# Ordering the residual's renewal behind the last transposed-row difference in a two-layer hybrid decoder trunk

## The chip, the core and the metric

The kernel runs on one core of one Trainium2 chip. The metric is the device time of one launch in microseconds, and smaller is better. The kernel before the change takes 2078.81 us, the median of three runs (2078.62 to 2080.05).

## What is computed

The reference is a decoder trunk of two layers on one sequence of 512 tokens, 1024 wide. Each layer has three sub-layers: a feed-forward half step, a mixer, and another feed-forward half step. Every sub-layer has the same frame: its input rows are scaled and shifted by vectors that come from a conditioning vector, its output is gated and added to the residual, and the sum is normalised:

```
h = x * (1.0 + scale) + shift
y = swiglu(h, w1, w3, w2)            # or hybrid_mixer(h, ...)
x = layer_norm(ALPHA * x + weight * (1.0 + gate) * y, g, b)
```

The mixer projects h into the inputs of three head groups (sparse attention, a gated spatial unit, a state-space scan) and projects their joined outputs back. Every product of matrices is kept to float32 accuracy.

## The kernel before, in words

**Tiling.** The 512 tokens are four blocks of 128. The residual `x_sb` holds them with tokens on partitions. Matmuls want the contraction on partitions, so the scaled and shifted rows are kept transposed, and in two parts: `hT_hi`, rounded to the matmul's format, and `hT_lo`, the difference of the exact value and `hT_hi`. A float32 product is then three matmuls (`mm3`, L120 to L123): high by high, high by low, low by high. Weights are split in the same way after their load (L103 on ScalarE, L105 on VectorE).

**From one sub-layer to the next.** At the end of a sub-layer, each token block goes through `post_norm` (L247): the output is added to the residual and its statistics are taken (L244, L245, L258, L232, L233, L260), and ScalarE writes the normalised block into a buffer `z` (L269). `flush` (L272) hands `z` to `spread` (L209): TensorE transposes it in eight pieces of 128x128 into two PSUM banks `hps` (L215), ScalarE scales and shifts seven of the pieces (L226) and VectorE one (L224) into `hsum`, ScalarE rounds to `hT_hi` (L228), and VectorE takes the difference `hT_lo` (L229). There are two differences of 128x512 per block, so eight per sub-layer. This way leads straight from `z` to the next sub-layer's input; the layer norm's own gain and offset are folded into the scale and shift.

**The renewal.** The residual itself still needs the layer norm's gain and offset. `renew` (L278 to L282) does this on VectorE for each block: a product `x = z * lg` (L281) and a sum `x = x + lb` (L282), each 128x1024 in float32. `renew` is called once at the end of a sub-layer, in the feed-forward step (L404) and in the mixer (L1026). The last sub-layer has none; it writes the output. So there are five boundaries between sub-layers, with 4 products and 4 sums each. The renewed residual is read again only when the next sub-layer's output is added to it.

**What sets the order.** A tile scheduler orders the instructions of each engine when the program is built, by dependences and priorities. Each engine then works off its list in order, and so does each queue of transfers. Where nothing says otherwise, the scheduler may put the renewal of one block between the steps of the others.

**The start of a mixer** (L460 to L486). For each of the four token blocks, two products go into two PSUM banks, `tA` (L465, 24 matmuls of 284 columns) and `tB` (L469, 24 matmuls of 256 columns). These banks come from a pool with three banks, taken in turn: the first block's `tA` and `tB` and the second block's `tA` have one each; the second block's `tB` takes the bank of the first `tA`, and the third block's `tA` takes the bank of the first `tB`. A bank can be taken again when its last reader is done. For `tB` that is the last step of the activation `gelu2`: ScalarE squares (L428), VectorE multiplies and adds (L429, L430), ScalarE takes tanh (L431), and VectorE writes `gv` (L432), reading `tB` once more. After the change VectorE's lines L429, L430, L432 are numbered L431, L432, L434.

**The start of a feed-forward step.** For each tile of the hidden width, two products `h` go into two PSUM banks. VectorE reads the first in L311 and the second in L312 (L313 and L314 after the change), which frees them for a later tile. VectorE also splits weights there (L105), reduces the next conditioning vectors (L156) and adds one to the gate `G` (L192). The buffers of `z`, `lg`, `lb` and `G` come from one pool of eight, and the load of the next `lg`, `lb` and `G` is issued on SyncE's queue when a buffer is free.

Of the kernel before, what the change touches and what calls it, by code (L numbers as in the profile page):

```python
# [10 lines left out]
F32 = mybir.dt.float32  # L11
# [40 lines left out]
def kernel(ctx: ExitStack, tc: tile.TileContext, a: dict, out: bass.AP,  # L52
                             subs=((0, 0), (0, 1), (0, 2), (1, 0), (1, 1), (1, 2))):
    nc = tc.nc
    V, S, G, PE = nc.vector, nc.scalar, nc.gpsimd, nc.tensor
# [18 lines left out]
    def slab(s, pool="s", dt=F32):  # L74
        return sp[pool].tile([128, 512], dt, tag=pool, name=nm(s))
# [8 lines left out]
    def bank(k, s):  # L84
        return psp[k].tile([128, 512], F32, tag=k, name=nm(s))
# [53 lines left out]
    hT_lo = const.tile([128, 4, 8, 128], F32R, name="hT_lo")  # L139
# [69 lines left out]
    def spread(b, z, P, banks):  # L209
        tiles = []  # L210
        for q in range(2):
            ps = bank(banks[q], "hps")
            for i in range(4):
                k = 4 * q + i
                PE.transpose(ps[:, i * 128:(i + 1) * 128], z[:, k * 128:(k + 1) * 128], ident)  # L215
            tiles.append(ps)
        for q in range(2):
            t = slab("hsum", "q")
            t3 = t.rearrange("p (k t) -> p k t", k=4)
            for i in range(4):  # L220
                sl = slice(i * 128, (i + 1) * 128)
                k = slice(4 * q + i, 4 * q + i + 1)
                if k.start in DVE_MOD:
                    V.tensor_scalar(t[:, sl], tiles[q][:, sl], P["GA"][:, k], P["BB"][:, k], op0=ALU.mult, op1=ALU.add)  # L224
                else:
                    S.activation(t[:, sl], tiles[q][:, sl], AF.Identity, bias=P["BB"][:, k], scale=P["GA"][:, k])  # L226
            hh = hT_hi[:, b, 4 * q:4 * q + 4, :]
            S.copy(hh, t3)  # L228
            V.tensor_sub(hT_lo[:, b, 4 * q:4 * q + 4, :], t3, hh.bitcast(F32))  # L229

    def rsqrt(dst, src, scale, eps, n):
        V.tensor_scalar(dst, src, scale, eps, op0=ALU.mult, op1=ALU.add)  # L232
# [39 lines left out]
    def flush(P, n=0):  # L272
        while len(P.get("z", [])) > n:
            b, z, banks = P["z"].pop(0)
            spread(b, z, P, banks)
            P.setdefault("zz", []).append((x_sb[:, b, :], z))

    def renew(P, n=0):  # L278
        while len(P.get("zz", [])) > n:
            x, z = P["zz"].pop(0)  # L280
            V.tensor_mul(x, z, P["lg"])  # L281
            V.tensor_add(x, x, P["lb"])  # L282

    def hT(t, b0, b1, k):
        return t[:, b0:b1, k, :]
# [11 lines left out]
    def ffn(l, s, P, last, bg, lead_order, params, feed=None):  # L297
# [21 lines left out]
        for half in range(2):  # L319
# [73 lines left out]
            for b in range(4):  # L393
# [6 lines left out]
                else:  # L400
                    flush(P)
                    post_norm(b, y[b], P, last, "YY")
        flush(P)
        renew(P)  # L404


# [27 lines left out]
    def mixer(l, P, last, lane, bg, gate_params, norm_params):  # L434
# [589 lines left out]
        tick(99)  # L1024
        flush(P)
        renew(P)  # L1026


# [90 lines left out]
    for n, (l, s) in enumerate(subs):  # L1119
        last = n == len(subs) - 1  # L1120
        P = {}
# [108 lines left out]
```

## Time and profile before

| what | value |
|---|---|
| median of three runs | 2078.81 us (2078.62 to 2080.05) |
| the profiled execution: its own time | 2078.53 us |
| the profiled execution: its span in the trace | 2076.8 us |
| TensorE (PE) busy | 2037.8 us, 98% |
| VectorE (DVE) busy | 1330.7 us, 64% |
| ScalarE (ACT) busy | 770.2 us, 37% |
| chain that ended last | PE 90%, DVE 5%, ACT 2%, issue 1%, DMA 1% |
| mean granted clock of PE | 0.998 |

The profiled execution took 2078.53 us; its trace spans 2076.8 us, and 1.7 us lie around it. In a row of the trace the engines are PE (TensorE matmul), PEld (weight load), DVE (VectorE), ACT (ScalarE), POOL (GpSimd) and SPq (SyncE's queue); L215 is line 215 of the kernel, and `hps<-cst,z` names what is written and what is read. In a timeline row the first number is the start, the second the duration, and square brackets give how long the engine stood idle before it, and for whom.

### The profile page before, as it was taken

Reading aid. Unit: us, or ns where it says so; the run is one execution under the profiler, and the core shown is the slowest. Engines: PE = TensorE matmul, PEld = TensorE weight load, DVE = VectorE, ACT = ScalarE, POOL = GpSimd, SP = SyncE. Lnnn points to the kernel's source line nnn. Section 1 sums busy time; section 2 is a strip of 40 time slices with the busy share of each in tenths; the row PEclk is TensorE's granted clock in tenths of the full one; section 3 lists DMA queues with packets and bytes.
Section 4 is the critical chain, followed back from the end, with each engine's and each line's share of the span. In section 5 each row is a group of like instructions: output and inputs, shape, how many; then the busy total and the mean of one; then the engine's idle time right before and its main releaser. Section 6 shows DMA issues by size and latency. Waiting matters only on the chain.

```text
span 2076.8 us, 25951 instructions
## 1 busy us (share of the span) xinstructions
PE 2037.8 (98%) x10024; PEld 1652.0 (80%) x10024; DVE 1330.7 (64%) x2425; ACT 770.2 (37%) x1352; POOL 27.8 (1%) x43
## 2 busy tenths in 40 slices
PE   6999999999999999999999999999999999999997
PEld 5888888887666888888888888888776678888886
DVE  6784455778898875334696534468788984444454
ACT  3321223525556422222343222235356673222322
POOL 0000000000000000000000000000000000000000
PEclk9999999999999999999999999999999999999999
DMA  9662633235353763332566333143254523233321
GB/s 359 225 232 83 213 122 124 74 99 173 126 169 92 260 201 108 93 100 61 172 231 185 93 100 98 65 144 102 92 172 129 176 79 125 81 112 93 100 92 41
DMA packets 93144, 280.26 MB, mean 135 GB/s; under 512 B 19251, under 2 KB 23603, under 8 KB 93020
## 3 DMA queue, kind: packets, MB, share of 16 engines
q1 hardware_dynamic: 92348, 275.95, 40.6%
q0 software_dynamic: 672, 2.64, 0.4%
q8 instruction: 79, 1.29, 0.3%
q14 instruction: 45, 0.37, 0.1%
HBM read 276.41 MB, written 4.76 MB: 135 GB/s over the span
## 4 chain that ended last, share of the span: by engine, by line
PE 90%; DVE 5%; ACT 2%; issue 1%; DMA 1%; POOL 0%; SPq 0%; POOLq 0%; ACTq 0%
PE h L121 15%; PE h L122 15%; PE h L123 15%; PE y L121 8%; PE y L123 8%; PE y L122 8%; PE pj L121 3%; PE pj L122 3%; PE pj L123 3%; PE op L931 3%; PE tp L921 2%; PE S L890 1%; DVE raw L156 1%; PE S L891 1%; PE hid L624 1%
## 5 line engine op out<-in xcount | busy, mean ns | idle before, releaser
L103 ACT CAST whi<-raw 128x1024 fp32r<-128x1024 f32 (+1 forms) x306 | 316.8, 1046 | 719.4 <-issue 353.8
L121 PE MATMUL h<-hT_hi,whi 128*128 128x512 f32 (+1 forms) x1488 | 559.1, 377 | 4.5 <-ACT hT_hi L1064 4.4
L122 PE MATMUL h<-hT_lo,whi 128*128 128x512 f32 (+1 forms) x1488 | 559.1, 376 | 0.0
L123 PE MATMUL h<-hT_hi,wlo 128*128 128x512 f32 (+1 forms) x1488 | 558.9, 376 | 0.0
L105 DVE TENSOR_TENSOR wlo<-raw,whi 128x1024 fp32r<-128x1024 f32 (+1 forms) x306 | 369.4, 1215 | 232.8 <-ACT whi L103 232.4
L121 PEld LDWEIGHTS h<-hT_hi,whi 128*128 128x128 f32 x1488 | 280.1, 188 | 56.0 <-ACT hT_hi L1064 5.4
L123 PEld LDWEIGHTS h<-hT_hi,wlo 128*128 128x128 f32 x1488 | 280.4, 188 | 50.8
L122 PEld LDWEIGHTS h<-hT_lo,whi 128*128 128x128 f32 x1488 | 280.5, 188 | 50.5 <-DVE hT_lo L1065 0.2
L121 PE MATMUL y<-whi,ghi 128*128 128x512 f32 x576 | 224.1, 389 | 0.0
L122 PE MATMUL y<-wlo,ghi 128*128 128x512 f32 x576 | 224.1, 389 | 0.0
L123 PE MATMUL y<-whi,glo 128*128 128x512 f32 x576 | 224.1, 389 | 0.0
L156 DVE CUSTOM_DVE_ANT_0 raw<-raw,csil 128x1024 f32<-128x1024 f32 x144 | 173.7, 1218 | 22.9 <-DMA raw<-in_ada_w_dram 22.4
L312 DVE TENSOR_TENSOR th<-th,h 128x512 f32<-128x512 f32 x88 | 60.2, 685 | 147.3 <-PE h L123 146.9
L101 DVE TENSOR_TENSOR raw<-raw,G 128x1024 f32<-128x1024 f32 x86 | 104.9, 1221 | 66.8 <-DMA raw<-in_w_dram 66.3
L123 PEld LDWEIGHTS y<-whi,glo 128*128 128x128 f32 x576 | 108.1, 188 | 22.5
L121 PEld LDWEIGHTS y<-whi,ghi 128*128 128x128 f32 x576 | 108.1, 188 | 22.5
L122 PEld LDWEIGHTS y<-wlo,ghi 128*128 128x128 f32 x576 | 108.1, 188 | 22.4
L121 PE MATMUL pj<-hT_hi,whi 128*128 128x512 f32 x288 | 117.3, 407 | 0.0
L122 PE MATMUL pj<-hT_lo,whi 128*128 128x512 f32 x288 | 113.7, 395 | 0.0
L123 PE MATMUL pj<-hT_hi,wlo 128*128 128x512 f32 x288 | 113.3, 393 | 0.0
L315 ACT CAST ghi<-th 128x512 fp32r<-128x512 f32 x88 | 54.5, 620 | 145.7 <-DVE th L312 145.7
L311 DVE SCALAR_TENSOR_TENSOR th<-th,h 128x512 f32<-128x512 f32 x88 | 59.9, 681 | 44.9 <-ACT th L310 44.8
(291 smaller groups left out, 2552.4 us busy)
## 6 DMA issues: line engine op xcount, KB each, us to landing
raw<-in_w_dram SPq DMA_DIRECT2D x264, 512.0 KB, 3.6
raw<-in_ada_w_dram SPq DMA_DIRECT2D x144, 512.0 KB, 5.5
raw<-in_wS_dram SPq DMA_DIRECT2D x36, 512.0 KB, 3.5
raw<-in_cw_dram SPq DMA_DIRECT2D x16, 512.0 KB, 3.7
raw<-in_wo_dram SPq DMA_DIRECT2D x16, 512.0 KB, 4.2
T<-lane SPq DMA_DIRECT2D x16, 256.0 KB, 3.7
lg<-in_ln_g_dram SPq DMA_DIRECT2D x6, 512.0 KB, 4.6
lb<-in_ln_b_dram SPq DMA_DIRECT2D x6, 512.0 KB, 3.8
```

What stands on the lines that cost most here:

```text
L101: V.tensor_mul(raw, raw, gain)
L103: S.copy(hi[:, :n], raw[:, :n])
L105: V.tensor_sub(lo[:, :n], raw[:, :n], hi[:, :n].bitcast(F32))
L121: PE.matmul(o, lh, rh, start=first, stop=False)
L122: PE.matmul(o, lh, rl, start=False, stop=False)
L123: PE.matmul(o, ll, rh, start=False, stop=last)
L156: V.tensor_tensor_reduce(out=raw, in0=raw, in1=cond["c"], scale=0.5, scalar=0.0, op0=ALU.mult, op1=ALU.add, accum_out=acc[:, k:k + 1])
L311: V.scalar_tensor_tensor(th, th, 1.0, h1, op0=ALU.add, op1=ALU.mult)
L312: freed[0] = V.tensor_mul(th, th, h3).ins
L315: S.copy(hi, th)
L921: PE.transpose(tp[0:n, e * 128:(e + 1) * 128], pr[e][:, kb * 128:kb * 128 + n], ident)
L931: PE.matmul(op[r, :], v, pt[0:n, g * 256:(g + 1) * 256], start=(br == 0), stop=(br == 2 and kb == qb))
```

## The change

The difference L229 now leaves its instruction in `P["turned"]`, so that after the last block the entry is the last difference of the sub-layer. `renew` puts its products and sums inside `tc.issue_after(P["turned"])`: in the order that the scheduler writes for VectorE they all stand behind that instruction. What is computed is the same, and no instruction is added.

```
-            V.tensor_sub(hT_lo[:, b, 4 * q:4 * q + 4, :], t3, hh.bitcast(F32))
+            P["turned"] = V.tensor_sub(hT_lo[:, b, 4 * q:4 * q + 4, :], t3, hh.bitcast(F32)).ins
...
     def renew(P, n=0):
-        while len(P.get("zz", [])) > n:
-            x, z = P["zz"].pop(0)
-            V.tensor_mul(x, z, P["lg"])
-            V.tensor_add(x, x, P["lb"])
+        if len(P.get("zz", [])) > n:
+            with tc.issue_after(P["turned"]):
+                while len(P["zz"]) > n:
+                    x, z = P["zz"].pop(0)
+                    V.tensor_mul(x, z, P["lg"])
+                    V.tensor_add(x, x, P["lb"])
```

VectorE's order at the start of the first layer's mixer, before. The numbers behind names count buffers: `z_2616`, `z_2676`, `z_2736` and `z_2796` are the four normalised blocks, `hsum_2823` is the second half of the last of them, and `gv_2881` with `tB_2885` belongs to the mixer's first token block.

```order
L281 TENSOR_TENSOR x_sb<-z_2736,lg_493 128x1024
L258 BN_AGGR mv_2795<-st_2794 128x2
L282 TENSOR_TENSOR x_sb<-x_sb,lb_494 128x1024
...
L281 TENSOR_TENSOR x_sb<-z_2796,lg_493 128x1024
L229 TENSOR_TENSOR hT_lo<-hsum_2787,hT_hi 128x512
L282 TENSOR_TENSOR x_sb<-x_sb,lb_494 128x1024
L229 TENSOR_TENSOR hT_lo<-hsum_2816,hT_hi 128x512
L224 TENSOR_SCALAR hsum_2823<-hps_2811,GA_1645,BB_1646 128x128
...
L229 TENSOR_TENSOR hT_lo<-hsum_2823,hT_hi 128x512
L432 SCALAR_TENSOR_TENSOR gv_2881<-gl_2938,tB_2885 128x256
```

The same place in the changed kernel:

```order
L229 TENSOR_TENSOR hT_lo<-hsum_2823,hT_hi 128x512
L283 TENSOR_TENSOR x_sb<-z_2616,lg_493 128x1024
L283 TENSOR_TENSOR x_sb<-z_2676,lg_493 128x1024
L284 TENSOR_TENSOR x_sb<-x_sb,lb_494 128x1024 x2
L283 TENSOR_TENSOR x_sb<-z_2736,lg_493 128x1024
L283 TENSOR_TENSOR x_sb<-z_2796,lg_493 128x1024
L284 TENSOR_TENSOR x_sb<-x_sb,lb_494 128x1024 x2
L434 SCALAR_TENSOR_TENSOR gv_2881<-gl_2938,tB_2885 128x256
```

The renewals of the four blocks, which stood between the steps of the normalisation and the differences, now stand in one piece behind the last difference, and ahead of the instruction that frees the first block's `tB`.

TensorE's order at the same place, as the difference of the two kernels (`y_2327` is the last output of the feed-forward step, `tA_2884` the mixer's first product, `z_2736` the third normalised block):

```order
 L122 MATMUL y_2327<-wsl_2585,ghi_2302 128x512
 L123 MATMUL y_2327<-wsh_2583,glo_2303 128x512
+L215 MATMUL hps_2770<-cst,z_2736 128x128 x4
+L215 MATMUL hps_2775<-cst,z_2736 128x128 x4
 L121 MATMUL tA_2884<-whi_2849,hT_hi 128x284
 L122 MATMUL tA_2884<-wlo_2851,hT_hi 128x284
...
-L215 MATMUL hps_2770<-cst,z_2736 128x128 x4
-L215 MATMUL hps_2775<-cst,z_2736 128x128 x4
```

The transposes of the third block move ahead of the first nine matmuls of `tA`.

VectorE's order at the start of the first layer's second feed-forward step, in the changed kernel (`hsum_5838` is the second half of the last block, `th_6085` with `h_1080_5877` and `h_1081_5878` the first hidden tile):

```order
L229 TENSOR_TENSOR hT_lo<-hsum_5838,hT_hi 128x512
L283 TENSOR_TENSOR x_sb<-z_5373,lg_4611 128x1024
L283 TENSOR_TENSOR x_sb<-z_5616,lg_4611 128x1024
L284 TENSOR_TENSOR x_sb<-x_sb,lb_4612 128x1024 x2
L283 TENSOR_TENSOR x_sb<-z_5749,lg_4611 128x1024
L283 TENSOR_TENSOR x_sb<-z_5811,lg_4611 128x1024
L284 TENSOR_TENSOR x_sb<-x_sb,lb_4612 128x1024 x2
L105 TENSOR_TENSOR wlo_6083<-raw_6079,whi_6081 128x1024
L313 SCALAR_TENSOR_TENSOR th_6085<-th_6085,h_1080_5877 128x512
L192 TENSOR_SCALAR G_6107<-G_6107 128x1024
L314 TENSOR_TENSOR th_6085<-th_6085,h_1081_5878 128x512
```

Before, none of the eight renewals stood behind the last difference here; `G` came directly behind it, and L312 followed five instructions later. GpSimd's order does not change.

## Rows read from the trace of the kernel before

**Rows 1.** The page, part 1: busy time, share of the span, instructions.

```profile
PE 2037.8 (98%) x10024; PEld 1652.0 (80%) x10024; DVE 1330.7 (64%) x2425; ACT 770.2 (37%) x1352; POOL 27.8 (1%) x43
```

**Rows 2.** Waits of PE: total us, times, longest us.

```profile
PE hps L215 <- ACT z L269: 4.1, 5, 1.4
```

**Rows 3.** Timeline of PE, first layer's mixer start (start, duration, engine, line).

```profile
386.00 0.29 PE L121 MATMUL tA<-whi,hT_hi 128*128 128x284 f32 x1
...
388.73 1.09 PE L215 MATMUL hps<-cst,z 128*128 128x128 f32 x8 [1.40 <-ACT z L269]
...
393.67 1.09 PE L215 MATMUL hps<-cst,z 128*128 128x128 f32 x8
...
401.55 0.30 PE L121 MATMUL tA<-whi,hT_hi 128*128 128x284 f32 x1
```

**Rows 4.** Timeline of DVE, the same stretch.

```profile
388.70 1.23 DVE L281 TENSOR_TENSOR x_sb<-z,lg 128x1024 f32<-128x1024 f32 x1
389.84 0.20 DVE L258 BATCH_NORM_AGGREGATE mv<-st 128x2 f32<-128x12 f32 x1
...
398.72 0.69 DVE L229 TENSOR_TENSOR hT_lo<-hsum,hT_hi 128x512 fp32r<-128x512 f32 x1
399.33 0.41 DVE L432 SCALAR_TENSOR_TENSOR gv<-gl,tB 128x256 f32<-128x256 f32 x1
```

**Rows 5.** Timeline of ACT, the same stretch.

```profile
389.42 1.86 ACT L226 ACTIVATE hsum<-hps,BB,GA 128x128 f32<-128x128 f32 x5 [0.52 <-PE hps L215]
```

**Rows 6.** The two renewal lines: count, shortest/median/longest ns, first and last start.

```profile
L281 DVE TENSOR_TENSOR x_sb<-z,lg x20: 1212/1224/1227, 372.1 to 1710.8; 128x1024 f32<-128x1024 f32 x20
...
L282 DVE TENSOR_TENSOR x_sb<-x_sb,lb x20: 1193/1214/1226, 373.8 to 1712.0; 128x1024 f32<-128x1024 f32 x20
```

**Rows 7.** Timeline of PE, second layer's mixer start.

```profile
1409.18 0.29 PE L121 MATMUL tA<-whi,hT_hi 128*128 128x284 f32 x1
...
1411.62 1.09 PE L215 MATMUL hps<-cst,z 128*128 128x128 f32 x8 [1.11 <-ACT z L269]
...
1424.44 0.30 PE L121 MATMUL tA<-whi,hT_hi 128*128 128x284 f32 x1
```

**Rows 8.** Windows at the end: stretch, length, PE, PEld, DVE, ACT, POOL, PEclk, DMA, GB/s.

```profile
2063.00:2064.00 1.00, 0.95 (x5) 0.45 (x3) 0.34 (x3) 0.07 (x1) 0.55 (x1) 1.00 0.23 86
...
2066.00:2067.00 1.00, 0.00 (x0) 0.00 (x0) 1.00 (x3) 0.00 (x0) 0.00 (x0) 0.86 0.00 0
2067.00:2068.00 1.00, 0.00 (x0) 0.00 (x0) 1.00 (x2) 0.00 (x0) 0.00 (x0) 0.50 0.22 82
```

**Rows 9.** Timeline of PE at the kernel's start.

```profile
15.39 1.22 PE L121 MATMUL h<-hT_hi,whi 128*128 128x512 f32 x2 [1.14 <-ACT hT_hi L1064]
...
17.69 0.63 PE L123 MATMUL h<-hT_hi,wlo 128*128 128x512 f32 x1
18.12 0.63 PE L121 MATMUL h<-hT_hi,whi 128*128 128x512 f32 x1
...
19.08 0.39 PE L121 MATMUL h<-hT_hi,whi 128*128 128x512 f32 x1
19.31 0.40 PE L122 MATMUL h<-hT_lo,whi 128*128 128x512 f32 x1
...
22.73 1.21 PE L121 MATMUL h<-hT_hi,whi 128*128 128x512 f32 x4 [2.35 <-ACT hT_hi L1064]
```

**Rows 10.** Timeline of PE, starts of the feed-forward steps behind the first mixer.

```profile
688.49 1.09 PE L215 MATMUL hps<-cst,z 128*128 128x128 f32 x8 [0.27 <-ACT z L269]
...
710.01 0.39 PE L121 MATMUL h<-hT_hi,whi 128*128 128x512 f32 x1
...
1046.15 1.09 PE L215 MATMUL hps<-cst,z 128*128 128x128 f32 x8 [1.09 <-ACT z L269]
```

**Rows 11.** Timeline of DVE, first layer's second feed-forward start.

```profile
694.58 0.69 DVE L229 TENSOR_TENSOR hT_lo<-hsum,hT_hi 128x512 fp32r<-128x512 f32 x1 [0.69 <-ACT hT_hi L228]
```

**Rows 12.** The page, part 6: a load's issue count, KB, us to landing.

```profile
lg<-in_ln_g_dram SPq DMA_DIRECT2D x6, 512.0 KB, 4.6
```

## The prediction, made before the changed kernel ran

> **What bounds the kernel now.** I read the page's busy times first: TensorE works 98% of the span [rows 1], so a change on VectorE can gain only where TensorE stands still for it, and can lose wherever it makes TensorE stand still. Then I read the waits of TensorE. Those that the renewal can touch are the transposes that wait for a normalised block: 4.1 us in five waits [rows 2], one at each boundary between sub-layers. The timelines of the boundaries show why: VectorE has a renewal of 1.22 us [rows 6] between the steps of the normalisation, so that `z` comes late. At the first mixer's start TensorE idles 1.40 us for it [rows 3], at the second mixer 1.11 us [rows 7], at the feed-forward start in the second layer 1.09 us [rows 10]; about 0.5 us is left for the other two, of which 0.27 us stands in the row at 688.49 [rows 10].
>
> **The change, part by part.** Nothing is added or removed: 20 products and 20 sums move, eight at each of five boundaries, all on VectorE; no transfer is moved by hand. Where they overlap, one starts 1.14 us behind the other (388.70 to 389.84 [rows 4]), so a piece of eight takes 8 x 1.14 = 9.1 us (by their full durations 9.8 us [rows 6]). The question is who is queued behind that piece.
>
> *First mixer.* Behind the piece stands `gv` (L432 before), the last reader of the first block's `tB` bank, and the third block's `tA` takes that bank. Before, `gv` ended at 399.33 + 0.41 = 399.74 [rows 4] and the third block began at 401.55 [rows 3], so the bank was free 1.8 us ahead of need. In the changed kernel:
> - TensorE turns the third normalised block right behind the last output, at 386.00, where `tA` began [rows 3], without the wait.
> - ScalarE began to scale that block at 389.42 [rows 5], 0.69 us behind the transposes at 388.73 [rows 3]; now at about 386.7. The last difference began at 398.72 [rows 4], 9.30 us behind the scaling. I keep that distance, since ScalarE's work on the two blocks and TensorE's matmuls between their transposes are the same: 386.7 + 9.3 = 396.0, done 0.6 us later (the next instruction started 0.61 us behind it [rows 4]), 396.6.
> - The piece: 396.6 + 9.1 = 405.7. Then `gv`, 0.41 us: 406.1, and the bank is free for TensorE at about 406.2.
> - Without a wait TensorE would have wanted it at 401.55 - 1.40 = 400.15 or a little sooner. So it stands still some 6 us, and the third block starts 406.2 - 401.55 = 4.65 us later than before.
>
> Nothing gives this back: TensorE has no other work ahead of that matmul, and the blocks behind follow in order. While it waits VectorE and ScalarE catch up, so I see no second wait behind it.
>
> *Second mixer.* The same list, later. `tA` began at 1409.18, the third block at 1424.44 [rows 7]. With the same distances, 1409.18 + (406.2 - 386.0) = 1429.4, which is 4.95 us later. Together **+9.6 us**.
>
> *The clock.* At the end of the kernel TensorE's last matmul ends at about 2063.95, and the granted clock is still 1.00 of full speed in the next microseconds, 0.86 in the stretch 2066 to 2067 and 0.50 (1.2 GHz) in the next [rows 8]: it fell some 2.8 us after TensorE had stopped. A gap of 2.35 us at the kernel's start did not bring it down: the matmuls behind it last no longer than before it [rows 9]. The two new gaps of 6 us are above both. What a slow stretch costs is bounded by the kernel's start, where matmuls of 512 columns came 0.43 us apart (17.69, 18.12) from 15.39 to about 18.5 and later 0.23 us apart (19.08, 19.31) [rows 9]: 3.2 us at about half speed, which loses 1.5 us. Whether the state there is the one of the tail, the rows don't say. Between nothing (the clock stays) and 1.5 us per gap I take 1.5, the nearest row being the tail's: **+3.0 us**, bounds 0 and 3.0. The Trainium skill, "TensorE: Matmul & The Clock Gate", section "What's actually happening", says that the throttled clock is the default and activity releases it, which the fall in the tail bears out; it also says that the warm-up's penalty is under 1% of a typical span and that one should not fit to a specific count of slow matmuls. Leaving the term out by that advice would give 2086.3.
>
> *The three feed-forward starts.* Here the bubbles go: 1.09 + 0.5 us, and with each the refill (a matmul lasts 0.39 us but the next starts 0.23 us behind it [rows 9], 0.16 us lost at each of three): **-2.1 us**. The piece of eight is covered. The last difference began at 694.58 [rows 11]; in the changed kernel it begins there at the latest, so the renewals end by 695.2 + 9.1 = 704.3. Behind them stand one weight split of the renewal's size, L313, `G` and L314 (1.2 us and three of some 0.65, estimates from the renewal's and the difference's rows), which ends at about 707.5; the hidden bank that L314 frees is wanted at 710.01 [rows 10]. That leaves 2.5 us. If that cover were gone, TensorE would stand still by what is missing.
>
> *The sum.* 4.65 + 4.95 + 3.0 - 2.1 = +10.5 us on the profiled execution's own 2078.53 us, 2089.0 us. The median of the runs lies 0.28 us above that execution: **2089.3 us**.
>
> **The rivals.**
>
> *A: the clock stays, or falls too late to cost.* The stalls come as worked out, without the 3.0 us: **2086.3 us**. For it: the gap of 2.35 us left the clock alone, and the tail shows the fall only once, behind the very end of TensorE's work. Against it: there the fall came after 2.8 us, half of the gap that I expect. Chance 0.23.
>
> *B: the feed-forward starts turn late as well.* Ahead of L314 stands `G`, whose load is issued on SyncE's queue behind those of `lg` and `lb`, and these wait for buffers that the renewals free. If the load goes out only when the renewals end at 704.3 and takes 4.6 us, as the load of `lg` does [rows 12], `G` lands at 708.9, L192 and L314 add some 1.3 us, and L314 ends at 710.2: about the 710.01 at which TensorE wants the bank. The turning point is a landing at 708.7. Two loads in a row ahead of it would add up to 2 us at each of three starts: **2089.3 + 6 = 2095.3 us** at most, 2093 in the middle. Against it: a normalised block's buffer comes free with its product, not with its sum, and the first two products come first. Chance 0.10.
>
> *C: faster.* The piece of eight isn't in TensorE's way, since it is done by the time that the third block wants its bank, at 400.15. Then all five bubbles go: 1.40 + 1.11 + 1.09 + 0.5 = 4.1, with 0.16 us of refill each 4.9 us, and 2078.53 - 4.9 + 0.28 = **2073.9 us**. It decides when the last difference begins by 400.15 - 0.4 - 9.1 - 0.6 = 390.0; by the distances above it begins at 396.0, and only ScalarE's work on two blocks in half the time would bring that. Chance 0.04.
>
> *D: nothing to be measured.* The two stalls come to what the three bubbles give back, 2.1 us, and the clock stays: **2078.8 us**. Each stall would have to be some 1 us in place of 4.8, so the piece of eight would have to take about 5.3 us, where the rows give 9.1 to 9.8, or the last difference to come 3.7 us sooner. That the change doesn't do what it says is excluded by the order, in which the eight stand in one piece. Chance 0.06.
>
> **How the numbers follow.** The forecast has 0.57. About 0.2% of the time, 4.2 us, is what a measurement of this kernel can tell from no change; the forecast, A and B all lie above 2083.0, together 0.90; D is within it, 0.06; C is faster, 0.04. The range: below, A with stalls 1.4 us shorter each (the last difference earlier, when VectorE has nothing between) gives 2083.5; above, B in the middle with the longer piece (9.8 us in place of 9.1, twice 0.7) gives 2094.5. It leaves out C, D and the ends of A and B.
>
> **What would show it.** In the changed kernel's trace: at each mixer's start a gap of some 6 us on TensorE ahead of the third block's `tA`, put down to VectorE's `gv`; eight renewals in a piece of about 9 us ahead of `gv`; behind the gap a granted clock of about 0.5 for some 3 us; the waits of the transposes for `z` nearly gone; no new wait of `h` for L314. It would be wrong if `gv` ended by 400 there, or if the gap were near 2 us; a clock of 1.00 behind the gap would speak for A, and a wait of `h` at 710 for B.

## The result, and the profile after

The changed kernel takes 2093.43 us, the median of six runs (2091.68 to 2094.28), against 2078.82 us of six runs before: 1.0069 times as long, with a 95% interval of 1.0058 to 1.0080. It is slower by 14.6 us; 2089.3 us were forecast, with a range to 2094.5 us. The profiled execution has a span of 2090.5 us, 13.7 us more than before.

TensorE's busy time in the page, to be read beside [rows 1], is 4.1 us longer, although no matmul was added (the same work took longer somewhere):

```profile
PE 2041.9 (98%) x10024; PEld 1655.6 (79%) x10024; DVE 1334.9 (64%) x2425; ACT 769.6 (37%) x1352; POOL 25.1 (1%) x43
```

The waits of TensorE (total, times, longest) have a new largest entry behind the kernel's start, and the entry of [rows 2] is halved, not gone:

```profile
PE tA L121 <- DVE gv L434: 11.9, 2, 6.0
...
PE hps L215 <- ACT z L269: 2.0, 3, 1.0
...
PE hps L215 <- DVE x_sb L244: 0.9, 2, 0.4
```

TensorE's timeline at the first mixer's start, to be read beside [rows 3]: the third block's transposes come at 386.12 without a wait, the fourth block's at 391.12, and then the third token block's `tA` stands still for 5.97 us and begins at 406.33. Before it began at 401.55.

```profile
386.12 1.03 PE L215 MATMUL hps<-cst,z 128*128 128x128 f32 x8
391.12 1.09 PE L215 MATMUL hps<-cst,z 128*128 128x128 f32 x8
394.20 0.30 PE L121 MATMUL tA<-whi,hT_hi 128*128 128x284 f32 x1
406.33 0.61 PE L121 MATMUL tA<-whi,hT_hi 128*128 128x284 f32 x1 [5.97 <-DVE gv L434]
413.86 0.30 PE L121 MATMUL tA<-whi,hT_hi 128*128 128x284 f32 x1
```

VectorE's timeline of the same stretch, beside [rows 4], shows the piece of eight renewals from 396.78 to the start of `gv` at 405.86:

```profile
396.17 0.69 DVE L229 TENSOR_TENSOR hT_lo<-hsum,hT_hi 128x512 fp32r<-128x512 f32 x1
396.78 2.36 DVE L283 TENSOR_TENSOR x_sb<-z,lg 128x1024 f32<-128x1024 f32 x2
399.05 2.35 DVE L284 TENSOR_TENSOR x_sb<-x_sb,lb 128x1024 f32<-128x1024 f32 x2
401.32 2.36 DVE L283 TENSOR_TENSOR x_sb<-z,lg 128x1024 f32<-128x1024 f32 x2
403.59 2.36 DVE L284 TENSOR_TENSOR x_sb<-x_sb,lb 128x1024 f32<-128x1024 f32 x2
405.86 0.42 DVE L434 SCALAR_TENSOR_TENSOR gv<-gl,tB 128x256 f32<-128x256 f32 x1
```

The windows (stretch, length, busy shares of PE, PEld, DVE, ACT and POOL with instruction counts, granted clock, DMA share, GB/s) show the clock in that gap. It falls to 0.50 of full speed (1.2 GHz) while TensorE stands still, is still there when TensorE goes on, and rises again near 409.5:

```profile
401.00:402.00 1.00, 0.00 (x0) 0.00 (x0) 1.00 (x2) 0.00 (x0) 0.00 (x0) 1.00 0.00 0
402.00:403.00 1.00, 0.00 (x0) 0.00 (x0) 1.00 (x2) 0.00 (x0) 0.00 (x0) 0.83 0.00 0
403.00:404.00 1.00, 0.00 (x0) 0.00 (x0) 1.00 (x2) 0.00 (x0) 0.00 (x0) 0.50 0.00 0
...
408.00:409.00 1.00, 1.00 (x6) 1.00 (x6) 0.93 (x3) 0.00 (x0) 0.00 (x0) 0.50 0.00 0
409.00:410.00 1.00, 1.00 (x8) 1.00 (x7) 0.10 (x1) 0.00 (x0) 0.00 (x0) 0.76 0.00 0
410.00:411.00 1.00, 1.00 (x10) 1.00 (x9) 0.00 (x0) 0.00 (x0) 0.00 (x0) 1.00 0.00 0
```

Six matmuls fall into a microsecond there in place of ten. The third block takes 413.86 - 406.33 = 7.53 us; before it took 6.00 us, from 401.55 [rows 3] to the start of the fourth block in the trace of before:

```profile
407.55 0.30 PE L121 MATMUL tA<-whi,hT_hi 128*128 128x284 f32 x1
```

At the second mixer's start the same gap is there, and one that was to go is still there: the fourth block's transposes wait 1.03 us for `z`. The third block takes 1443.58 - 1435.17 = 8.41 us, 2.4 us more than the 6.00 us at full speed. The clock falls in this gap too, and it rises again near 1440.3, 5.1 us after TensorE went on; at the first start it rose after 3.1 us.

```profile
1419.97 1.09 PE L215 MATMUL hps<-cst,z 128*128 128x128 f32 x8 [1.03 <-ACT z L269]
1435.17 0.61 PE L121 MATMUL tA<-whi,hT_hi 128*128 128x284 f32 x1 [5.97 <-DVE gv L434]
1443.58 0.30 PE L121 MATMUL tA<-whi,hT_hi 128*128 128x284 f32 x1
```

```profile
1433.00:1434.00 1.00, 0.00 (x0) 0.00 (x0) 1.00 (x2) 0.00 (x0) 0.00 (x0) 0.74 0.00 0
...
1440.00:1441.00 1.00, 1.00 (x9) 1.00 (x8) 0.10 (x1) 0.00 (x0) 0.00 (x0) 0.85 0.00 0
```

**Where the time went.** The same VectorE instructions can be found in both traces, and how much later each starts, taken from one anchor to the next, gives the time that a stretch lost or won. The anchors are the first L244 behind 365 us, the fourth block's `dtx` at each mixer's start, the L311 near 798 and near 1163 us (times of the kernel before), and the last L244. The first column is the sum of the prediction's own terms; the others are traces (in us, - is sooner). A kernel's start differs from run to run by up to 1.5 us and is left out.

| stretch | forecast | changed | feed-forward starts only | mixer starts only | half | filled | behind gv | best version |
|---|---|---|---|---|---|---|---|---|
| start of the first mixer | +6.15 | +6.18 | 0.00 | +7.16 | +2.92 | +5.00 | +4.46 | -1.01 |
| its rest, and the start behind it | -0.4 | -0.05 | +0.18 | -0.36 | +0.09 | +0.64 | +0.33 | -0.01 |
| between the two feed-forward steps | -1.25 | -1.37 | -1.37 | +0.01 | -1.28 | -1.29 | -1.29 | -1.29 |
| start of the second mixer | +6.45 | +8.26 | +0.02 | +8.22 | +4.44 | +4.94 | +5.18 | -0.77 |
| its rest, and all behind it | -0.4 | +0.59 | +0.80 | -0.04 | +2.02 | +0.51 | +0.62 | +0.07 |

### The profile page after: what moved, and what is told of

The parts are those of the page before. It is cut to its first block, busy times and chain, and to the rows that moved or that the text cites. A ratio compares the mean times of both kernels' runs of the same rounds, so it can differ in the third digit from the quotient of the medians.

```text
span 2090.5 us, 25957 instructions
## 1 busy us (share of the span) xinstructions
PE 2041.9 (98%) x10024; PEld 1655.6 (79%) x10024; DVE 1334.9 (64%) x2425; ACT 769.6 (37%) x1352; POOL 25.1 (1%) x43
## 3 DMA queue, kind: packets, MB, share of 16 engines
q8 instruction: 79, 1.29, 0.2%
## 4 chain that ended last, share of the span: by engine, by line
PE 91%; DVE 5%; ACT 2%; DMA 1%; issue 1%; POOL 0%; SPq 0%; POOLq 0%; ACTq 0%
PE h L121 15%; PE h L123 15%; PE h L122 15%; PE y L121 8%; PE y L123 8%; PE y L122 8%; PE pj L121 3%; PE pj L122 3%; PE pj L123 3%; PE op L933 3%; PE tp L923 2%; PE S L892 1%; DVE raw L156 1%; PE S L893 1%; PE hid L626 1%; ACT hsum L226 1%
## 5 line engine op out<-in xcount | busy, mean ns | idle before, releaser
L314 DVE TENSOR_TENSOR th<-th,h 128x512 f32<-128x512 f32 x88 | 60.2, 685 | 145.7 <-PE h L123 145.1
```

What stands on the lines that cost most here:

```text
L314: freed[0] = V.tensor_mul(th, th, h3).ins
```

## The experiments

My theory after this: the loss is made at the two mixer starts, by TensorE waiting for a bank whose reader stands behind the piece, and by the clock behind that wait. Rivals: the renewals cost time wherever they are held back (late loads, late work at the feed-forward starts); the loss goes in proportion to what is held back; the third block is slow for another reason than the clock.

### Only the starts of the feed-forward steps

```
-            with tc.issue_after(P["turned"]):
+            behind = tc.issue_after(P["turned"]) if not P["to_mixer"] and P.get("zz") else nullcontext()
+            with behind:
```

> The renewal stands behind the last difference only at the three boundaries that lead into a feed-forward step; at the two mixer starts it is free, as before the change. Theory (the loss is made at the mixer starts, by gv waiting behind eight renewals): what is left of the change is its effect at the feed-forward starts, read from the drift of VectorE's L312 between the two traces as 0, -1.4 and +0.35 us, so 2077.8 us (2076.8 to 2079.0). Rival (late loads and a late L314 at the feed-forward starts take part in the loss): 2082 us or more.

Measured: 2078.94 us against 2079.22 us, ratio 1.0000 (0.9991 to 1.0009). The stretches of the mixer starts are as before (0.00 and +0.02 us), the boundary between the two feed-forward steps gives 1.37 us, and the rest gives it back. So the order costs nothing measurable at the three feed-forward starts, though VectorE's first step on a hidden tile comes some 4 to 5 us late at two of them. The gain is not resolved by the times; by its trace's stretches it is 0.4 us, less than the 1.0 us that I had read from the changed kernel.

### Only the starts of the mixers

```
+            behind = tc.issue_after(P["turned"]) if P["to_mixer"] and P.get("zz") else nullcontext()
```

> The reverse: the renewal stands behind the last difference only at the two mixer starts. Theory: the whole loss and none of the small gain, 2093.4 + 1.0 = 2094.4 us (2092.5 to 2096); the gap ahead of the third block's tA is about 6.0 us at both starts. Rival (the loss is spread over the boundaries): below 2090 us.

Measured: 2092.71 us (2092.41 to 2094.16), ratio 1.0065 (1.0048 to 1.0082), a little under the expected 2094.4 but inside the bounds that were given. The two gaps are 5.96 us each. With the run before it, this places the loss: it is at the mixer starts, all of it.

### Half the piece

With `one()` for the product and the sum of one block:

```
+        while P["to_mixer"] and len(P.get("zz", [])) > 2:
+            one()
+        if P.get("zz"):
+            with tc.issue_after(P["turned"]):
+                while P["zz"]:
+                    one()
```

> At the mixer starts only the renewals of the last two blocks stand behind the last difference, a piece of 4 x 1.14 = 4.6 us in place of 9.1; the other two are free, as before the change. The feed-forward starts are as in the changed kernel. Theory (a threshold: the piece costs only what goes beyond the time that TensorE wants the bank, and a short gap leaves the clock alone): gv ends some 4.5 us sooner than in the changed kernel, the gap ahead of the third block is about 1 us at each start, the granted clock stays at 1.00, 2079.8 us (2078.5 to 2081.5). Rival (the loss goes in proportion to the renewals that are held back): half of 14.6 us, 2086.1 us.

Measured: 2087.36 us (2087.07 to 2087.83), ratio 1.0040 (1.0025 to 1.0055). My number was wrong by 7.6 us, and the rival's 2086.1 was near. The trace shows why, and that it is not a proportion either: the waits of both starts are 2.6 us, not 1.

```profile
405.25 0.40 PE L122 MATMUL tA<-whi,hT_hi 128*128 128x284 f32 x1 [2.62 <-DVE gv L440]
```

```profile
1429.88 0.40 PE L122 MATMUL tA<-whi,hT_hi 128*128 128x284 f32 x1 [2.63 <-DVE gv L440]
```

I had let the piece shrink by 4.5 us and kept the last difference where the full piece has it (396.17). But the two free renewals bring back the bubble of 1.40 us and the late `z`: the last difference begins at 399.63 here. Halving the piece moved its end by 1.1 us only (`gv` at 404.78 in place of 405.86), or by 1.9 us when this run's later start is taken off. The time that TensorE wants the bank comes later by the bubble, so the gap is shorter, but the third block starts at 405.25, 2.8 us later than before when this run's later start (0.90 us against the kernel before) is taken off. Then the clock: equal gaps, and in the windows it stays at 1.00 at the first start, while at the second it falls behind the gap, when TensorE has been at work again for over a microsecond:

```profile
405.00:406.00 1.00, 0.75 (x5) 0.75 (x6) 1.00 (x5) 0.52 (x3) 0.00 (x0) 1.00 0.00 0
406.00:407.00 1.00, 1.00 (x10) 1.00 (x9) 0.52 (x3) 0.42 (x1) 0.00 (x0) 1.00 0.00 0
...
1430.00:1431.00 1.00, 1.00 (x8) 1.00 (x9) 1.00 (x4) 0.45 (x3) 0.00 (x0) 1.00 0.00 0
1431.00:1432.00 1.00, 1.00 (x8) 1.00 (x7) 0.48 (x2) 0.42 (x1) 0.00 (x0) 0.71 0.09 16
1432.00:1433.00 1.00, 1.00 (x6) 1.00 (x5) 0.61 (x2) 0.00 (x0) 0.00 (x0) 0.50 0.00 0
```

That accounts for 4.44 us at the second start against 2.92 us at the first. Another 1.0 us is a new wait far behind (TensorE for VectorE in the gated unit, at 1540 us), which no other run here has; I did not follow it.

### Filling the gap

Added, ahead of the third block's `tA`, into a bank that nothing reads (and that `tA` is ordered behind the last of them):

```
+            if b == 2:
+                filler = bank("P", "filler")
+                with tc.issue_after(tail[0]):
+                    for i in range(24):
+                        fill = PE.matmul(filler, hT_hi[:, 0, 0, :], wb[0][0][:, 0:512], start=True, stop=True).ins
```

> The changed kernel with 24 matmuls of 512 columns added ahead of the third block's tA at each mixer start, into a PSUM bank that nothing reads; they fill 24 x 0.23 = 5.5 us of the gap of 6.0. Nothing else is changed. Theory (behind the gap the clock costs 1.5 us at the first and 2.4 us at the second mixer start): gv and so the third block come at the same time as in the changed kernel, the granted clock stays at 1.00, and the third block takes 6.0 us in place of 7.5 and 8.4: 2093.4 - 3.9 = 2089.5 us (2088.3 to 2090.7). Rival (the third block is slow for another reason, the clock does not matter): 2093.4 us. If the added matmuls delay TensorE themselves, the time is above 2093.4 us.

Measured: 2087.69 us (2087.15 to 2089.67), ratio 1.0043 (1.0028 to 1.0058): 5.7 us less than the changed kernel, although TensorE does 48 matmuls more, and below the range that was given. The wait of TensorE for `gv` is 1.0 us in all:

```profile
PE tA L122 <- DVE gv L435: 1.0, 2, 0.5
```

The third block starts at 406.23 as in the changed kernel, and the clock stays at 1.00 there. The two starts lose 5.00 and 4.94 us, close to the forecast's 4.65 and 4.95 us, which hold no term for the clock. Of the 5.7 us, the first start gives 6.18 - 5.00 = 1.2, the second 8.26 - 4.94 = 3.3, of which some 0.9 is the gap ahead of the fourth block's transposes, which this run happened not to have: the wait of `al` for its load, to which that gap is traced below, was 1.58 us here in place of 2.57. So the clock cost about 1.2 + 2.4 = 3.6 us in the changed kernel's trace. The two profiled executions are 4.1 us apart (2092.24 and 2088.10 us); that the medians are 5.7 us apart comes from the spread of the runs, since the one lies 1.2 us below its median and the other 0.4 us above.

### The piece behind gv

The renewals of a mixer start are written behind the first block's `gelu2`, and `renew` orders them behind its `gv` with `tc.issue_after(ready)`:

```
+            ready = gelu2(dst, tb[:, :256], 256)
+            if b == 0:
+                old = put_off.pop()
+                old["ready"] = ready
+                renew(old)
```

> The changed kernel, but at the mixer starts the piece of eight renewals stands behind gv of the first token block in place of ahead of it (it is written there in the program and ordered behind that instruction). Theory (TensorE waits for whatever bank reader stands behind the piece): the wait of the third block's tA for gv is gone; the third block's tB takes the bank of the second tA, whose reader on VectorE (dtx) stands behind the piece now; gv ends at about 397.2, the piece at 406.3, and tB would be wanted at 403.3, so the gap is about 3.1 us, half of 6.0, and stands ahead of tB. 2082.7 us if the clock stays, up to 2086.2 us if it falls at both starts. Rival (only gv mattered, and the renewals are free behind it): no gap, 2076.2 us.

Measured: 2088.43 us (2087.99 to 2089.23), ratio 1.0045 (1.0030 to 1.0060). The mechanism is the one expected and the size is not. The wait for `gv` is gone, and a new one stands ahead of the third block's `tB`, 3.79 us in place of 3.1:

```profile
407.79 0.58 PE L122 MATMUL tB<-whi,hT_hi 128*128 128x256 f32 x1 [3.79 <-ACT vW L486]
```

It is put down to ScalarE's copy `vW`, which I had not counted. ScalarE's timeline shows what stands behind what: `gts` waits 5.92 us for VectorE's `dtx`, and the two copies that read the same bank follow in order.

```profile
407.22 0.19 ACT L484 ACTIVATE gts<-tA 128x24 f32<-128x24 f32 x1 [5.92 <-DVE dtx L483]
407.30 0.26 ACT L485 COPY vS<-tA 128x128 f32<-128x128 f32 x1
407.45 0.28 ACT L486 COPY vW<-tA 128x128 f32<-128x128 f32 x1
```

`gts` reads other columns of `tA` than `dtx`, and nothing that `dtx` writes. The Trainium skill, "PSUM — Partial Sum Buffer", section "PSUM bank collisions raise a hardware error", says that the compiler's scheduler adds a dependency between two instructions of different engines that touch the same 32 partitions of one bank, two readers included; the wait of 5.92 us in this row agrees with it, though no run shows what put the wait there. The two longer gaps are 1.4 us of the 2.2 us by which the time lies above the upper number of the expectation. The clock is not the rest of it: it fell at both starts, but the third block's `tB` took 4.41 and 4.47 us in place of 2.87, so it cost 1.5 and 1.6 us, where I had allowed up to 1.75 at each. What the trace shows besides is that TensorE still waits for `z` ahead of the transposes, 0.58 us at the first and 1.01 us at the second start.

### The gap at the second mixer start, two runs

In the changed kernel the load of the mixer's parameters lands at about 1415.6 us. Two instructions wait for it ahead of the fourth block's normalisation: `cw` on VectorE (0.66 us) and `al` on ScalarE (2.57 us). In the changed kernel's trace:

```profile
1415.62 0.21 ACT L652 ACTIVATE al<-p 128x4 f32<-128x4 f32 x1 [2.57 <-DMA p<-in_p_dram]
1415.62 0.18 DVE L491 TENSOR_SCALAR cw<-p 128x30 f32<-128x30 f32 x1 [0.66 <-DMA p<-in_p_dram]
```

First `cw` alone was moved behind the last difference (`turned[0]`), then `al` too, behind the last rounding (`rounded[0]`).

```
+        with tc.issue_after(turned[0]):
             V.tensor_scalar(cw, p2[:, 416:446], 0.5, None, op0=ALU.mult)
...
+        with tc.issue_after(rounded[0]):
             S.activation(al, alog, AF.Exp)
```

> The changed kernel with one small instruction moved: the scaling of the convolution's weights (cw, 128x30), which waited for a load of 0.66 us more at the second mixer start and stood between the two halves of the last block's statistics, is ordered behind the last difference. Theory (that wait made z late and left a gap of 1.03 us ahead of the transposes there): that gap falls under 0.3 us, the third block starts there some 0.9 us sooner, the gaps of 6.0 us ahead of it stay, 2092.5 us, to be read from the trace more than from the time. Rival (z is late for another reason): the gap of 1.0 us stays, 2093.4 us.

Measured: 2093.08 us (2092.04 to 2094.33), and the gap stays:

```profile
1421.85 0.33 PE L217 MATMUL hps<-cst,z 128*128 128x128 f32 x1 [1.11 <-ACT z L272]
```

VectorE no longer waited for the load there, and `z` was as late as before: whatever the load does there, it does not do it through `cw`. The next run tells whether it does it through `al`.

> As the run with cw moved, and one more small instruction moved: ScalarE's al (an exponential of 128x4), which reads the same late load of parameters and stood in ScalarE's queue ahead of the scaling of the third block at the second mixer start (2.57 us of waiting there, to 1415.62 where the transposes would have let it go on at about 1414.7), is ordered behind the last rounding of the rows. Theory (the load holds ScalarE, not VectorE): the gap of 1.0 us ahead of the fourth block's transposes falls under 0.3 us, the two gaps of 6.0 us stay, some 0.9 us less than the changed kernel, 2092.5 us (2091 to 2094, since the clock's cost varies by more than that between runs). Rival: the gap of 1.0 us stays.

Measured: 2092.33 us (2090.39 to 2093.48), and the transposes' waits for `z` are 1.0 us over the whole kernel, none of them at a mixer start; the two gaps of 6.0 us stay.

```profile
PE tA L121 <- DVE gv L438: 11.9, 2, 6.0
...
PE hps L218 <- ACT z L273: 1.0, 2, 0.5
```

So ScalarE's `al` held the third block's scaling, and with it the fourth block's `z`. The times of these two runs overlap each other and the changed kernel's; only the traces tell them apart.

### A version that keeps the gain

At the mixer starts the renewals of two blocks stand behind the first block's `gv` and of two behind the second block's. At the boundary between two feed-forward steps they stand behind the last difference, and at the two boundaries from a mixer they are free, as before the change. `cw` is moved, and in the second of the two runs `al` too. `renew` takes two blocks from the list each time and orders them with `tc.issue_after(ready)`.

```
+            ready = gelu2(dst, tb[:, :256], 256)
+            put_off[0]["ready"] = ready
+            if b < 2:
+                renew(put_off[0], 2 - 2 * b)
```

> A version meant to keep the gain without the loss: at the mixer starts two renewals (2 x 2 instructions, 4.6 us) stand behind gv of the first token block and two behind gv of the second; at the one boundary between two feed-forward steps the renewals stand behind the last difference; at the two boundaries from a mixer to a feed-forward step they are free, as before the change; cw is ordered behind the last difference. Theory: each piece of four ends ahead of the next bank's turn (first piece at 401.8, its bank wanted at 403.3; second at 408.5, wanted at 409.4), so no gap on TensorE at the mixer starts, and the three bubbles of 1.40, 1.11 and 1.09 us with 0.16 us of refill each are gone: 2079.2 - 4.1 = 2075.1 us (2074.2 to 2076.5). Rival (VectorE's later work, which is held up by some 9 us, makes TensorE wait for split weights): 2078 us or more.

Measured: 2076.82 us (2076.08 to 2079.01) against 2079.19 us, ratio 0.9988 (0.9979 to 0.9998). It is faster than the kernel before, by less than the 4.1 us expected, and a little above the range that was given; 0.88 us of the gap at the second mixer start were still there.

> The version with two renewals behind each of the first two gv, and al moved in the same way. Theory: the gap of 0.88 us that this version still had at the second mixer start goes, 2076.8 - 0.9 = 2075.9 us (2075.0 to 2077.0), with an interval against the kernel before that lies below 1. Rival: the gap stays, 2076.8 us.

Measured: 2076.43 us (2075.57 to 2077.84) against 2079.28 us, ratio 0.9986 (0.9977 to 0.9995). The gain is 0.14%, less than the 0.2% that the prediction took for the least that can be told; but the slowest of its 11 runs is faster than the fastest of the 15 runs before (2078.43 us). No wait of the transposes for `z` is left at the mixer starts or between the feed-forward steps; what is left are the two of 0.3 us behind the mixers, and a new one of 0.4 us for `vW` at the end of each mixer start:

```profile
PE pj L122 <- ACT vW L490: 0.8, 2, 0.4
PE hps L219 <- ACT z L274: 0.5, 2, 0.3
```

The trace gives 1.01, 1.29 and 0.77 us at the three places, 3.1 us together, and the medians 2.85 us. I had expected 1.6 and 1.3 us at the mixer starts; the waits for `vW` take 0.42 us of each.

## Why the prediction was right, point by point

**The stall.** Right in place, cause and size. The last difference was to begin at 396.0, the bank to be free at 406.2 and the gap to be some 6 us; the trace has 396.17, 406.33 and 5.97 us. The run that fills the gap lost 5.00 and 4.94 us at the two starts, where the forecast had 4.65 and 4.95. Behind the gap the order of VectorE and ScalarE did catch up; no second wait came.

**The second mixer's start.** Mis-sized: I moved the first start's distances over, +4.95 us, and the third block came 5.84 us later there: 1435.17 against 1424.44 [rows 7] is 10.73 us, of which 4.89 us were there already when the last output ended (the transposes behind it start at 1414.07, where `tA` started at 1409.18 before). The step that failed is "with the same distances": the gap of 1.11 us did not go. Before, it stood for a late `z` behind renewals; with these out of the way, ScalarE's `al` waited for a load in the same place. The two runs that moved `cw` and `al` show it.

**The clock.** Right in kind, mis-sized: 3.0 us forecast, 1.5 and 2.4 us by the third block's length, about 3.6 us by the run that fills the gap. The 1.5 us that I took from the kernel's start holds for one gap and not as an upper bound: the slow clock lasted 3.1 us into the work at the first start and 5.1 us at the second. The Trainium skill, "TensorE: Matmul & The Clock Gate", section "HAM oscillation — how this bites in real kernels", says that a wait for data between pieces of work brings the clock down and lets the next piece start slow; the rows at 402 to 410 us agree, where the wait is for a bank. The advice that the prediction took from the Trainium skill, "TensorE: Matmul & The Clock Gate", section "What's actually happening", would have left the term out and given 2086.3 us; the measurement decides against that here.

One premise of the term does not hold from run to run. In the trace of before, a gap of 2.35 us at the kernel's start left the clock alone [rows 9], and gaps of 2.39 and 2.52 us at the same place did so in two other traces. But behind gaps of 1.91, 2.06 and 2.13 us there, in three more, the granted clock was 0.50. In the run with `cw` moved:

```profile
22.96 1.65 PE L121 MATMUL h<-hT_hi,whi 128*128 128x512 f32 x3 [2.13 <-ACT hT_hi L1070]
24.00:25.00 1.00, 1.00 (x4) 0.81 (x3) 1.00 (x3) 0.99 (x2) 0.00 (x0) 0.50 1.17 371
```

So the length of such a short gap does not tell whether the clock falls, and the 2.35 us were a weaker sign for A than they were taken for. All eight gaps of 6.0 us in the four traces that have them brought it down.

**The feed-forward starts.** Half right. No stall came, as forecast, and the one boundary between two feed-forward steps gave 1.37 us where 1.25 were forecast. The other two were to give 0.8 us together and gave nothing: the step that failed is that their waits for `z` were the renewals' doing. TensorE's waits there grew. Ahead of the transposes it waits 0.43 us for VectorE's L244 and 0.50 us for `z` behind the first mixer, and 0.43 and 0.49 us behind the second, where it had waited 0.27 and 0.26 us for `z`. VectorE's timeline of the changed kernel shows what took the free places, weight splits of the next step, each as long as a renewal, between the parts of the last block's statistics:

```profile
684.54 1.21 DVE L105 TENSOR_TENSOR wlo<-raw,whi 128x1024 fp32r<-128x1024 f32 x1
685.67 0.69 DVE L244 TENSOR_TENSOR x_sb<-y,x_sb 128x512 f32<-128x512 f32 x1
686.27 1.22 DVE L105 TENSOR_TENSOR wlo<-raw,whi 128x1024 fp32r<-128x1024 f32 x1
687.40 0.69 DVE L245 BATCH_NORM_STATS2 st<-x_sb 128x6 f32<-128x512 f32 x1
688.00 1.21 DVE L105 TENSOR_TENSOR wlo<-raw,whi 128x1024 fp32r<-128x1024 f32 x1
```

Three splits stand there, where before it was one split and one sum of a renewal, and from the first L244 to L258 these statistics take 7.4 us in place of 5.4. That the splits are what keeps `z` late is read from this order; no run moved them.

**The sum.** Forecast +10.5 us; the five stretches of the changed kernel's trace add up to 6.18 - 0.05 - 1.37 + 8.26 + 0.59 = 13.6 us. Of the 3.1 us between them, 1.8 are at the second mixer's start (0.9 for the gap that stayed, 0.9 for the clock) and 1.3 at the boundaries behind the mixers; the boundary between the feed-forward steps gave 0.1 more than forecast. Nearly all of it is on the slow side, so the time lies near the upper end of the range. That end is itself a little high: halfway between 2089.3 and 2095.3 us is 2092.3 and not 2093, which would make it 2093.7 us. The median lies inside by either.

**The rivals.** A, without the clock, is refuted by the windows and by the run that fills the gap. B is refuted: the first L314 behind the second mixer came 4 to 5 us later than the rest of the kernel there, and TensorE did not wait for it. C needed the piece to end by 400; it ended at 405.9. D needed stalls of 1 us; the gaps are 5.97 us.

## What to carry to other kernels

Work that is off the path still needs a place in its engine's order, and the question is not whether the engine has time for it but who stands behind it: here 9.1 us of VectorE work stood ahead of one 0.4-us reader that freed a PSUM bank. Find the first reader that the busiest engine waits for, and put the work behind it in pieces no longer than the time to the next one. When a cause of lateness is taken away, ask what moves into its place: an instruction waiting for a load did at one boundary, and weight splits, by the order, at two others.

## What was not expected of the hardware

- A TensorE that stands still costs more than the gap: behind two gaps of 5.97 us the next six microseconds of work took 1.5 and 2.4 us more, at a granted clock of 0.50 for the first 3.1 and 5.1 us of it. In four runs with the same gap at the first mixer start, the stretch lost 6.18, 7.16, 6.83 and 6.36 us.
- The fall can come behind the gap: of two equal gaps of 2.6 us in one run, one left the clock at 1.00, and behind the other it fell when TensorE had worked again for over a microsecond. At the kernel's start gaps of 1.91 to 2.13 us brought it down in three traces, and gaps of 2.35 to 2.52 us left it alone in three others.
- Adding 48 matmuls that compute nothing made the changed kernel 5.7 us faster by the medians; the traces put some 3.6 us of it to the clock.
